# Where TensorE's operands start in SBUF: a two-block transformer kernel on one Trainium2 core

## The chip, the core and the metric

The kernel runs on one core of one Trainium2 chip. Five engines work beside each other there: TensorE (PE in the profile; PEld is its weight load), VectorE (DVE), ScalarE (ACT), GpSimd (POOL) and the queue engine SyncE (SP), and transfers run on 16 DMA engines. The metric is the device time of one execution in microseconds; less is better. A difference of under 0.2% can't be told from no change here.

## What is computed

Two transformer blocks on 256 tokens of width 1024, in float32. The reference, cut to its skeleton:

```python
# block 1
h = rmsnorm(x, g1); parts = split(h @ w_in)            # 1024 -> 6416 columns
att = sliding_window_attention(q, k, v, sinks) @ w_branch_attn
hm = mlstm_chunkwise(...) @ w_branch_mlstm
x = x + (sigmoid(ga) * att + sigmoid(gm) * hm) @ w_out
x = x + peer_ffn(rmsnorm(x, g2), ...)                  # 128 of 16384 experts for each token
# block 2
p = split(rmsnorm(x, g3) @ w_in_2)                     # 1024 -> 5632 columns
x = x + (sigmoid(gs) * stick_breaking(p) + sigmoid(gh) * hgrn2(p)) @ w_out
hn = rmsnorm(x, g4)
x = x + (silu(hn @ w_gate) * (hn @ w_up)) @ w_down     # hidden width 2816
```

`peer_ffn` picks 16 experts for each of 8 heads and each token, takes the dot product of the token with the expert's row of `expert_down`, and adds up the rows of `expert_up` weighted by gate and gelu.

## The kernel before

**Dense products.** Every product with a weight matrix is made in three TensorE passes over operands in the format float32r: a float32 value is split into a rounded part (`hi`) and the rest (`lo`), and `mm3` (L119 to L125) adds up weights-lo times activations-hi, weights-hi times activations-lo and hi times hi. Each weight tile of 512 KB (128 partitions by 1024 values, 4096 bytes in each partition) goes through `stream` (L111): a DMA from SyncE's queue into `raw` (3 buffers), ScalarE rounds it into `hi` (4 buffers, L105), and VectorE or GpSimd, by a pattern of letters (`lo_pat`), writes `lo` (3 buffers, L109).

A matmul has two operands in SBUF: a stationary one of 128 columns, which a weight load puts into the array (the engine called PEld), and a moving one, which streams past it. The weights of the next matmul are loaded while the present one streams. There are two ways of using them:

- `proj_tok_steps` (token-major): the activations are stationary and the weights move, 512 columns a matmul. The profile names such a matmul `acc<-lo,T1h 128x512`. A weight tile has 12 of them. The stages are q, the values, `w_out`, the mixer's inputs of block 2, and the last product `w_fd`.
- `proj_feat_steps` (feature-major): the weights are stationary and the activations move, 256 columns a matmul. The profile names such a matmul `acc<-T1l,hi 128x256`. A weight tile has 24 of them. The stages are the gates, the branch products, the PEER query and the two first products of the FFN (`w_fg`, `w_fu`).

I call them wide (512 columns) and narrow (256 columns). The program has 1056 narrow ones on `fhTh`/`fhTl` (FFN), 1152 on `T1h`/`T1l` (six projections of 192 each, 1152 in all), 192 on `aTh`/`aTl`, 192 on `hmTh`/`hmTl` (the same memory, by tag), 192 on `rTh`/`rTl` (PEER query), and 192 on `oTh`/`oTl`: 2976. Of wide ones 264 have `fTh`/`fTl` stationary, the others `T1h`/`T1l`.

**The gather in the middle.** For PEER, `experts` (L780 on) gathers for one expert of all 128 tokens a tile `ga` (1 MB, 8192 bytes in each partition) by an indirect DMA of GpSimd, 256 times, into ten buffers. VectorE makes the dot product (L794), ScalarE a diagonal matrix `dg` (L800), and TensorE adds up `dg` times the second half of `ga` (L803, float32).

**Order and memory.** The instructions' order on each engine is set by the framework's scheduler from the program's order and priorities. Tiles come from pools; pools are laid out in SBUF one after another in the order in which they are opened, and tiles within a pool in the order of their first use. So the size of any tile moves all tiles that come after it. The built program gives these starts of the tiles in their partitions, in bytes modulo 256:

| tile | role | before | after the change |
|---|---|---|---|
| `hi`, `lo`, feature-major | stationary | 192 | 64 |
| `hi`, `lo`, token-major | moving | 192 | 0 |
| `T1h`, `T1l`, `fhTh`, `fhTl` | moving (narrow), stationary (wide) | 192 | 0 |
| `aTh`, `aTl`, `hmTh`, `hmTl` | moving (narrow) | 32 | 0 |
| `rTh`, `rTl` | moving (narrow) | 160 | 128 |
| `oTh`, `oTl` | moving (narrow) | 128 | 0 |
| `fTh`, `fTl` | stationary (wide) | 96 | 0 |
| `ga` / `dg` | moving / stationary of L803 | 160 / 160 | 0 / 0 |

Slices of these tiles start at multiples of 512 bytes from the tile's start.

Of the kernel before, what the change touches and what calls it, by code (L numbers as in the profile page):

```python
# [10 lines left out]
F32 = mybir.dt.float32  # L11
F32R = mybir.dt.float32r
# [9 lines left out]
P = 128  # L22
D = 1024
KD = D // P
# [6 lines left out]
W_O = (22, 23, 25)  # L31
RAWB, HIB, LOB = 3, 4, 3
NWARM = 9
EB, GB = 4, 10
PI2 = 2.0 * math.pi


# [2 lines left out]
for _n, _w in (("g1", 8), ("g2", 8), ("g3", 8), ("g4", 8), ("lb0", 4), ("lb1", 4), ("ib", 1), ("fb", 1),  # L40
               ("invf", 8), ("sink", 16), ("qg", 64), ("kg", 64), ("qg2", 64), ("kg2", 64), ("hg", 128)):
    _SM[_n] = (_o, _o + _w)
    _o += _w
SMW = _o


@with_exitstack
def peer_hybrid_kernel(ctx: ExitStack, tc: tile.TileContext, A: dict, out: bass.AP, dbg=None, stop=None):
# [15 lines left out]

    warm = st.tile([P, 512], BF, tag="lo", name="warm", bufs=LOB)
    V.memset(warm, 0.0)
    wa = kp.tile([P, 2], F32, name="wa")
    G.memset(wa, 0.0)
    S.activation(wa[:, 0:1], wa[:, 1:2], AF.Copy)
    x = kp.tile([P, 2, D], F32, name="x", tag="xs")  # L70
# [37 lines left out]
            cnt[0] += 1  # L108
        return (V if eng == "v" else G).tensor_tensor(dst_l, src, dst_h.bitcast(F32), op=ALU.subtract)  # L109

    def stream(src, n=1024):  # L111
        raw = st.tile([P, n], F32, tag="raw", name="raw", bufs=RAWB)
        hi = st.tile([P, n], F32R, tag="hi", name="hi", bufs=HIB)
        lo = st.tile([P, n], F32R, tag="lo", name="lo", bufs=LOB)
        with tc.high_priority(offset=PRIO):
            nc.sync.dma_start(raw, src)
            split(hi, lo, raw)
        return hi, lo
# [25 lines left out]
    def proj_feat_steps(w, n, xh, xl, KT, evac, nm=4, tag="acc", kc0=0):  # L144
        acc = [bank(tag) for _ in range((nm + 1) // 2)]
        kp_ = 8 // nm
        for kc in range(KT // kp_):
            hi, lo = stream(w[n, kc0 + kc])
            hi = hi.rearrange("p (k n) -> p k n", k=kp_)
            lo = lo.rearrange("p (k n) -> p k n", k=kp_)  # L150
            for m in range(nm):
                o = acc[m // 2][:, (m % 2) * 256:(m % 2) * 256 + 256]
                ms = slice(m * P, m * P + P)
                for k2 in range(kp_):
                    k = kc * kp_ + k2
                    mm3(o, hi[:, k2, ms], lo[:, k2, ms], xh[:, k], xl[:, k], k == 0 and m % 2 == 0,
                        k == KT - 1 and (m % 2 == 1 or m == nm - 1))
            if kc < KT // kp_ - 1:
                yield
        for m2 in range(len(acc)):  # L160
            evac(m2, acc[m2])
        yield
# [161 lines left out]
    with ExitStack() as c1:  # L324
# [5 lines left out]
        def ten(shape, name, bufs=1, dt=F32, tag=None):  # L330
            return b1.tile(shape, dt, tag=tag or name, name=name, bufs=bufs)

        hTh, hTl = t1()
        n1 = Norm(x, par("g1"), b1, hTh, hTl, ("s4", 3))
        n1.half(0)
# [128 lines left out]
        dump("kT", kT)  # L464


        attTh = ten([P, KD, 256], "aTh", dt=F32R)
        attTl = ten([P, KD, 256], "aTl", dt=F32R)
        nsink = ten([P, 16], "nsink")
        V.tensor_scalar(nsink, par("sink"), -1.0, None, op0=ALU.mult)  # L470
        for tt in range(2):
# [191 lines left out]


    with ExitStack() as c2:
        wp = c2.enter_context(tc.tile_pool(name="wp", bufs=1))
        gp = c2.enter_context(tc.tile_pool(name="gp", bufs=1))
        lo_pat[0] = "p"
        keys = wp.tile([P, 8, P], F32, name="keys")
        nc.scalar.dma_start(keys, A["peer_keys"])  # L670
# [111 lines left out]
        def experts(tt, h, r0, EB):  # L782

            if uacc[tt][0] is None:
                uacc[tt] = [bank("acc") for _ in range(2)]
            s_ = gp.tile([P, EB], F32, name="s_", bufs=3)
            dg = gp.tile([P, EB, P], F32, name="dg", bufs=2)
            rows = []
            for j in range(EB):
                ga = gp.tile([P, 2 * D], F32, name="ga", bufs=GB)  # L790
                G.indirect_dma_start(ga, None, A["peer_du"], bass.IndirectOffsetOnAxis(  # L791
                    idx[tt][h][:, r0 + j:r0 + j + 1], 0))
                jk = gp.tile([P, D], BF, name="jk", bufs=1)
                dot = V.scalar_tensor_tensor(jk, ga[:, 0:D], 1.0, xn[:, tt], op0=ALU.mult, op1=ALU.mult,  # L794
                                             accum_out=s_[:, j:j + 1])
                rows.append(ga)
            S.activation(s_, s_, AF.Gelu)
            V.tensor_tensor(s_, s_, gate[tt][h][:, r0:r0 + EB], op=ALU.mult)
            for j in range(EB):
                S.activation(dg[:, j], ident, AF.Copy, scale=s_[:, j:j + 1])  # L800
            for dh in range(2):
                for j in range(EB):
                    T.matmul(uacc[tt][dh], dg[:, j], rows[j][:, D + dh * 512:D + dh * 512 + 512],  # L803
                             start=h + r0 + j == 0, stop=h == 7 and r0 + j == 15)
            return dot
# [28 lines left out]
    with ExitStack() as c4:  # L834
        b2 = c4.enter_context(tc.tile_pool(name="b2", bufs=1))

        def ten(shape, name, bufs=1, dt=F32, tag=None):
            return b2.tile(shape, dt, tag=tag or name, name=name, bufs=bufs)

        def head_norm2(src, nh, hd, gain, tag):  # L840
            sv = src.rearrange("p (h d) -> p h d", h=nh)
# [55 lines left out]
        qs, ks, vs = (ten([P, 2, 512], nm_) for nm_ in ("qs", "ks", "vs"))  # L897
        vh = ten([P, 2, 512], "vh", tag="qs")
        gg = ten([P, 2, 512], "gg", tag="ks")
        oTh = ten([P, KD, 256], "oTh", dt=F32R)  # L900
        oTl = ten([P, KD, 256], "oTl", dt=F32R)
        qT2 = ten([P, 4, 256], "qT2")
        kT2 = ten([P, 4, 256], "kT2")
        attn = ten([P, 2, 4, P], "attn")
# [197 lines left out]
    with ExitStack() as c5:  # L1102
        fp = c5.enter_context(tc.tile_pool(name="fp", bufs=1))
        hTh = fp.tile([P, KD, 256], F32R, name="fhTh")
        hTl = fp.tile([P, KD, 256], F32R, name="fhTl")
        n4 = Norm(x, par("g4"), fp, hTh, hTl)
        for n in range(2):
            cs_ = slice(n * 512, (n + 1) * 512)
# [2 lines left out]
            n4.half(n)  # L1111
        n4.factor(row=False)
        dump("x4", x)
        NF = 22
        fTh = fp.tile([P, NF, 256], F32R, name="fTh")
        fTl = fp.tile([P, NF, 256], F32R, name="fTl")
        for n in range(6):
            nm = 4 if n < 5 else 2
            got = []
# [113 lines left out]
```

## Time and profile before

| | us |
|---|---|
| median of 3 runs (lowest, highest) | 1396.51 (1396.5, 1397.77) |
| the profiled execution | 1393.9 |
| its span, first to last instruction | 1392.1 |
| TensorE busy | 1228.3 (88%) |
| VectorE / GpSimd / ScalarE busy | 891.0 / 567.7 / 515.3 |

The profiled execution's time is 1.8 us more than its span, and 2.6 us less than the median of the runs. A matmul's duration in the profile is the time from its start to the end of its result, and matmuls overlap: the next one starts long before the former ends. What counts in a run of matmuls is the time from one start to the next, which I call the pitch. It is worked out from a view that counts the instructions in a stretch: since those that stick out at the stretch's edges are counted too, the pitch is (stretch + one duration) / count.

### The profile page before, as it was taken

The numbers are of one execution on the slowest core, as the hardware profiler recorded it, in microseconds if no ns is written. First come the engines' busy times: TensorE is split into PE (matmuls) and PEld (weight loads), VectorE is DVE, ScalarE is ACT, GpSimd is POOL, SyncE is SP. The second block draws the span as 40 slices with busy tenths as digits, with TensorE's granted clock in tenths as the row PEclk, the third lists the DMA queues.
The fourth block names the chain that finished last, engine by engine and source line by source line (L and its number), as shares of the span: only waits on it lengthen the run. The fifth ranks groups of instructions, "written<-read, shape, count | busy, mean of one in ns | idle before, by whom it ended". The sixth has DMA issues, their size and how long they took to land.

```text
span 1392.1 us, 16704 instructions
## 1 busy us (share of the span) xinstructions
PE 1228.3 (88%) x5785; PEld 849.9 (61%) x5785; DVE 891.0 (64%) x1963; ACT 515.3 (37%) x927; POOL 567.7 (41%) x394
## 2 busy tenths in 40 slices
PE   8999999994888777878777786878999999999998
PEld 6976789993333333333333332333888999899987
DVE  6966658558576776666867766665699786442521
ACT  6465434452122222112322211221474564544442
POOL 3321412543535444444434454453100005578764
PEclk9999999995889889989988999999999999999999
DMA  6543325666999999999999999999355335465564
GB/s 215 168 134 107 121 92 169 186 191 265 421 421 421 419 421 416 421 419 412 408 419 419 416 422 411 415 409 411 116 163 167 106 107 181 153 189 176 188 190 136
DMA packets 69779, 383.53 MB, mean 276 GB/s; under 512 B 8000, under 2 KB 8512, under 8 KB 36928
## 3 DMA queue, kind: packets, MB, share of 16 engines
q0 software_dynamic: 36864, 268.45, 46.8%
q1 hardware_dynamic: 31968, 112.11, 26.1%
q10 hardware_dynamic: 864, 1.90, 0.4%
q8 instruction: 46, 0.75, 0.2%
q14 instruction: 37, 0.30, 0.1%
HBM read 381.39 MB, written 1.05 MB: 275 GB/s over the span
## 4 chain that ended last, share of the span: by engine, by line
PE 45%; DMA 24%; DVE 16%; issue 7%; POOL 6%; ACT 1%; POOLq 0%; SPq 0%; ACTq 0%; DVEq 0%
DMA ga<-in_peer_du_dram,idx 22%; PE acc L121 11%; PE acc L124 11%; PE acc L125 10%; POOL ga L791 5%; DVE jk L794 5%; PE acc L803 2%; PE sm L124 2%; PE sm L125 2%; PE sm L121 2%; PE sm L489 1%; PE sm L1052 1%; PE s L514 1%; DVE lo L109 1%; ACT hi L105 1%
## 5 line engine op out<-in xcount | busy, mean ns | idle before, releaser
L803 PE MATMUL acc<-ga,dg 128*128 128x512 f32 x1024 | 509.3, 657 | 145.1 <-ACT dg L800 144.9
L803 PEld LDWEIGHTS acc<-ga,dg 128*128 128x128 f32 x1024 | 210.6, 210 | 442.7 <-issue 252.8
L791 POOL DMA_INDIRECT ga<-in_peer_du_dram,idx x256 | 297.3, 1161 | 361.7 <-PE acc L803 236.6
L794 DVE SCALAR_TENSOR_TENSOR jk<-ga,xn 128x1024 bf16<-128x1024 f32 x256 | 313.4, 1224 | 199.9 <-DMA ga<-in_peer_du_dram,idx 199.6
L109 POOL TENSOR_TENSOR lo<-raw,hi 128x1024 fp32r<-128x1024 f32 (+1 forms) x88 | 216.8, 2467 | 392.9 <-PE acc L125 258.2
L105 ACT ACTIVATE hi<-raw 128x1024 fp32r<-128x1024 f32 (+1 forms) x210 | 220.3, 1051 | 256.6 <-PE acc L125 75.2
L109 DVE TENSOR_TENSOR lo<-raw,hi 128x1024 fp32r<-128x1024 f32 (+1 forms) x122 | 157.8, 1294 | 105.4 <-PE acc L124 35.1
L121 PE MATMUL acc<-T1l,hi 128*128 128x256 f32 x384 | 109.8, 287 | 0.3 <-DVE T1l L237 0.3
L124 PE MATMUL acc<-T1h,lo 128*128 128x256 f32 x384 | 109.9, 286 | 0.0
L125 PE MATMUL acc<-T1h,hi 128*128 128x256 f32 x384 | 109.3, 285 | 0.0
L121 PE MATMUL acc<-lo,T1h 128*128 128x512 f32 (+1 forms) x256 | 99.8, 395 | 3.3 <-DVE lo L109 3.0
L124 PE MATMUL acc<-hi,T1l 128*128 128x512 f32 (+1 forms) x256 | 99.9, 391 | 0.7 <-DVE T1l L306 0.6
L125 PE MATMUL acc<-hi,T1h 128*128 128x512 f32 (+1 forms) x256 | 99.6, 390 | 0.0
L121 PEld LDWEIGHTS acc<-T1l,hi 128*128 128x128 f32 x384 | 73.3, 191 | 1.8 <-issue 0.7
L124 PEld LDWEIGHTS acc<-T1h,lo 128*128 128x128 f32 x384 | 73.4, 191 | 1.0 <-issue 0.5
L125 PEld LDWEIGHTS acc<-T1h,hi 128*128 128x128 f32 x384 | 73.4, 191 | 0.9 <-issue 0.4
L121 PEld LDWEIGHTS acc<-lo,T1h 128*128 128x128 f32 x256 | 48.7, 192 | 12.9 <-DVE lo L109 3.5
L124 PEld LDWEIGHTS acc<-hi,T1l 128*128 128x128 f32 x256 | 49.0, 191 | 11.9 <-DVE T1l L306 1.9
L125 PEld LDWEIGHTS acc<-hi,T1h 128*128 128x128 f32 x256 | 48.9, 191 | 10.2 <-issue 1.0
L125 PE MATMUL sm<-fhTh,hi 128*128 128x256 f32 x176 | 49.6, 283 | 0.0
L124 PE MATMUL sm<-fhTh,lo 128*128 128x256 f32 x176 | 49.6, 283 | 0.0
L124 PE MATMUL acc<-fhTh,lo 128*128 128x256 f32 x176 | 49.6, 283 | 0.0
(849 smaller groups left out, 1995.1 us busy)
## 6 DMA issues: line engine op xcount, KB each, us to landing
raw<-in_w_in_dram SPq DMA_DIRECT2D x92, 512.0 KB, 3.5
raw<-in_w_fg_dram SPq DMA_DIRECT2D x22, 512.0 KB, 3.6
raw<-in_w_fu_dram SPq DMA_DIRECT2D x22, 512.0 KB, 3.7
raw<-in_w_fd_dram SPq DMA_DIRECT2D x22, 512.0 KB, 3.8
raw<-in_w_out_dram SPq DMA_DIRECT2D x16, 512.0 KB, 3.6
raw<-in_w_ba_dram SPq DMA_DIRECT2D x8, 512.0 KB, 3.5
raw<-in_w_bm_dram SPq DMA_DIRECT2D x8, 512.0 KB, 4.0
raw<-in_peer_wq_dram SPq DMA_DIRECT2D x8, 512.0 KB, 3.5
```

The source lines that it names most:

```text
L105: S.activation(dst_h, src, AF.Copy)
L109: return (V if eng == "v" else G).tensor_tensor(dst_l, src, dst_h.bitcast(F32), op=ALU.subtract)
L121: m = T.matmul(o, lh, rl, start=start, stop=False)
L124: T.matmul(o, ll, rh, start=False, stop=False)
L125: return T.matmul(o, lh, rh, start=False, stop=stop)
L489: T.matmul(b[:, (i - i0) * W:(i - i0 + 1) * W], qT[pr, h // 2, tt * P:(tt + 1) * P], kT[pr, g, 0:W], start=False, stop=i == i0 + per - 1)
L514: T.matmul(po[pr, :], kv[:, sb, P + g * 64:P + g * 64 + 64], pT, start=sb == 0, stop=sb == tt)
L791: G.indirect_dma_start(ga, None, A["peer_du"], bass.IndirectOffsetOnAxis(idx[tt][h][:, r0 + j:r0 + j + 1], 0))
L794: dot = V.scalar_tensor_tensor(jk, ga[:, 0:D], 1.0, xn[:, tt], op0=ALU.mult, op1=ALU.mult, accum_out=s_[:, j:j + 1])
L803: T.matmul(uacc[tt][dh], dg[:, j], rows[j][:, D + dh * 512:D + dh * 512 + 512], start=h + r0 + j == 0, stop=h == 7 and r0 + j == 15)
L1052: T.matmul(b[:, tt * 4 + m], xl_[:, m, tt], xr_[:, m, tt, :, 1], start=tt + m == 0, stop=tt + m == 4)
```

## The change

It moves no work between engines, and adds none. It sets the byte positions of TensorE's operands:

- The tiles `wa` and `s_` are made 32 columns wide (only the first columns are used), and the parameter tile `sm` is rounded up to a multiple of 64 columns, so that the tiles behind them start at multiples of 256 bytes. `s_` gets a fourth buffer.
- `attTh`/`attTl`, `oTh`/`oTl` and `fTh`/`fTl` are allocated ahead of the other tiles of their pools, and the pool `gp` of the gather is opened ahead of `wp`.
- Each `hi` and `lo` buffer is 64 values (256 bytes) longer, and a feature-major product uses the part that starts 16 values, which is 64 bytes, behind the buffer's start.

```diff
-EB, GB = 4, 10
+EB, GB, OFF = 4, 10, 64
...
-SMW = _o
+SMW = -(-_o // 64) * 64
...
-    wa = kp.tile([P, 2], F32, name="wa")
+    wa = kp.tile([P, 32], F32, name="wa")
...
-    def stream(src, n=1024):
+    def stream(src, n=1024, shift=0):
         raw = st.tile([P, n], F32, tag="raw", name="raw", bufs=RAWB)
-        hi = st.tile([P, n], F32R, tag="hi", name="hi", bufs=HIB)
-        lo = st.tile([P, n], F32R, tag="lo", name="lo", bufs=LOB)
+        hi = st.tile([P, 1024 + OFF], F32R, tag="hi", name="hi", bufs=HIB)[:, shift:shift + n]
+        lo = st.tile([P, 1024 + OFF], F32R, tag="lo", name="lo", bufs=LOB)[:, shift:shift + n]
...
-            hi, lo = stream(w[n, kc0 + kc])
+            hi, lo = stream(w[n, kc0 + kc], shift=16)
...
+        attTh = ten([P, KD, 256], "aTh", dt=F32R)
+        attTl = ten([P, KD, 256], "aTl", dt=F32R)
...
+        gp = c2.enter_context(tc.tile_pool(name="gp", bufs=1))
         wp = c2.enter_context(tc.tile_pool(name="wp", bufs=1))
-        gp = c2.enter_context(tc.tile_pool(name="gp", bufs=1))
...
-            s_ = gp.tile([P, EB], F32, name="s_", bufs=3)
+            s_ = gp.tile([P, 32], F32, name="s_", bufs=4)[:, 0:EB]
...
+        oTh = ten([P, KD, 256], "oTh", dt=F32R)
+        oTl = ten([P, KD, 256], "oTl", dt=F32R)
...
+        NF = 22
+        fTh = fp.tile([P, NF, 256], F32R, name="fTh")
+        fTl = fp.tile([P, NF, 256], F32R, name="fTl")
```

TensorE's instructions stand in the same order as before throughout; so do GpSimd's and SyncE's. Near the start, where the cosines of the rotary embedding (`cs`) are made, the scheduler exchanges some rows on VectorE and ScalarE. On ScalarE, where `T1h` are the last parts of the first normed activations, `junk,nss` the squares for their norm, and `hi` the first weight tiles, it stands thus before:

```order
L218 ACTIVATE T1h<-sm 128x256 x2
L105 ACTIVATE hi<-raw 128x1024
L218 ACTIVATE T1h<-sm 128x256
L243 ACTIVATE junk,nss<-x 128x512 x3
L396 ACT_TABLE_LOAD
L396 ACTIVATE cs<-ang 128x32
L243 ACTIVATE junk,nss<-x 128x512
```

And in the changed kernel (its lines are two to four higher there):

```order
L220 ACTIVATE T1h<-sm 128x256 x2
L106 ACTIVATE hi<-raw 128x1024
L400 ACT_TABLE_LOAD
L400 ACTIVATE cs<-ang 128x32
L220 ACTIVATE T1h<-sm 128x256
L245 ACTIVATE junk,nss<-x 128x512 x4
```

The table load and the cosines have moved ahead of the last part of `T1h`.

## Rows read from the trace of the kernel before

**Rows 1.** The page: busy time, and the span in 40 slices.

```profile
PE 1228.3 (88%) x5785; PEld 849.9 (61%) x5785; DVE 891.0 (64%) x1963; ACT 515.3 (37%) x927; POOL 567.7 (41%) x394
...
PE   8999999994888777878777786878999999999998
...
PEclk9999999995889889989988999999999999999999
DMA  6543325666999999999999999999355335465564
```

**Rows 2.** The page: chain that ended last, first line, and the gather's DMA queue.

```profile
q0 software_dynamic: 36864, 268.45, 46.8%
...
PE 45%; DMA 24%; DVE 16%; issue 7%; POOL 6%; ACT 1%; POOLq 0%; SPq 0%; ACTq 0%; DVEq 0%
```

**Rows 3.** Stretches: each engine's busy us and count, granted clock, DMA share, GB/s.

```profile
core 0: us, PE busy (x) PEld busy (x) DVE busy (x) ACT busy (x) POOL busy (x), PEclk, DMA share, GB/s
141.00:189.00 48.00, 46.76 (x290) 36.01 (x288) 27.11 (x39) 19.93 (x34) 16.36 (x7) 1.00 0.33 100
244.00:266.00 22.00, 22.00 (x186) 22.00 (x185) 9.86 (x12) 10.03 (x11) 9.14 (x4) 1.00 0.57 175
309.00:315.00 6.00, 6.00 (x53) 6.00 (x52) 5.93 (x7) 4.04 (x5) 0.00 (x0) 1.00 0.37 120
400.00:900.00 500.00, 392.19 (x802) 162.59 (x801) 341.19 (x913) 113.69 (x310) 230.67 (x199) 0.91 1.01 417
999.00:1008.00 9.00, 9.00 (x77) 9.00 (x76) 5.39 (x5) 5.00 (x6) 3.38 (x2) 1.00 0.57 177
1010.00:1025.00 15.00, 15.00 (x68) 12.43 (x67) 12.83 (x21) 11.54 (x13) 1.05 (x1) 1.00 0.57 163
1077.00:1149.00 72.00, 72.00 (x563) 67.63 (x562) 55.03 (x99) 40.41 (x48) 1.98 (x1) 1.00 0.36 109
1151.00:1171.00 20.00, 20.00 (x179) 20.00 (x178) 11.05 (x13) 9.02 (x11) 11.03 (x5) 1.00 0.60 190
1218.00:1326.00 108.00, 108.00 (x902) 108.00 (x901) 44.14 (x36) 49.79 (x57) 86.06 (x41) 1.00 0.58 183
1330.00:1386.00 56.00, 56.00 (x242) 45.05 (x241) 9.42 (x8) 19.11 (x18) 31.54 (x14) 1.00 0.56 169
```

**Rows 4.** Groups by form on PE: 1151 to 1171 us, then one of 1218 to 1326 us.

```profile
L121 PE MATMUL acc<-oTl,hi 128*128 128x256 f32 x60 | 16.6, 276 | 0.0
...
L124 PE MATMUL sm<-fhTh,lo 128*128 128x256 f32 x157 | 44.3, 283 | 0.0
```

**Rows 5.** Timeline of PE in order of time: start, us, instruction, [idle before <-releaser].

```profile
228.01 0.55 PE L275 MATMUL sm<-cst,hm 128*128 128x128 f32 x3 [0.99 <-DVE hm L655]
...
308.00 0.68 PE L261 MATMUL sm<-cst,nr 128*128 128x128 f32 x4 [1.09 <-DVE nr L195]
...
1207.39 0.28 PE L125 MATMUL acc<-fhTh,hi 128*128 128x256 f32 x1
1210.68 0.57 PE L261 MATMUL sm<-cst,nr 128*128 128x128 f32 x3 [3.02 <-DVE nr L195]
```

**Rows 6.** Groups by form on PE: the first of 1331 to 1351 us and of 1010 to 1025 us.

```profile
L124 PE MATMUL acc<-hi,fTl 128*128 128x512 f32 x29 | 11.6, 399 | 0.0
...
L124 PE MATMUL acc<-hi,T1l 128*128 128x512 f32 x23 | 9.0, 389 | 0.0
```

**Rows 7.** The page: GpSimd's lo group, and the landing time of FFN weights.

```profile
L109 POOL TENSOR_TENSOR lo<-raw,hi 128x1024 fp32r<-128x1024 f32 (+1 forms) x88 | 216.8, 2467 | 392.9 <-PE acc L125 258.2
...
raw<-in_w_fg_dram SPq DMA_DIRECT2D x22, 512.0 KB, 3.6
```

**Rows 8.** Timeline around 20 us: ScalarE, then VectorE, then PE.

```profile
18.17 0.47 ACT L218 ACTIVATE T1h<-sm 128x256 fp32r<-128x256 f32 x1
...
20.50 1.28 ACT L396 ACT_TABLE_LOAD   x1
21.79 0.23 ACT L396 ACTIVATE cs<-ang 128x32 f32<-128x32 f32 x1
...
20.57 0.47 DVE L219 SCALAR_TENSOR_TENSOR T1l<-sm,T1h 128x256 fp32r<-128x256 f32 x1
...
21.83 0.41 PE L121 MATMUL acc<-lo,T1h 128*128 128x272 f32 x2
```

More of the change, by code (lines that the diff above doesn't have):

```diff
@@ L464, in peer_hybrid_kernel @@
         dump("kT", kT)
-        attTh = ten([P, KD, 256], "aTh", dt=F32R)
-        attTl = ten([P, KD, 256], "aTl", dt=F32R)
         nsink = ten([P, 16], "nsink")
@@ L899, in peer_hybrid_kernel @@
         gg = ten([P, 2, 512], "gg", tag="ks")
-        oTh = ten([P, KD, 256], "oTh", dt=F32R)
-        oTl = ten([P, KD, 256], "oTl", dt=F32R)
         qT2 = ten([P, 4, 256], "qT2")
@@ L1113, in peer_hybrid_kernel @@
         dump("x4", x)
-        NF = 22
-        fTh = fp.tile([P, NF, 256], F32R, name="fTh")
-        fTl = fp.tile([P, NF, 256], F32R, name="fTl")
         for n in range(6):
```

## The prediction

> **What bounds the kernel now.** I read the page's busy line and slices first, then the chain, then a table of stretches. TensorE is busy for 88% of the span, and its slices show 9 except in the middle, where the DMA slices show 9 instead [rows 1]. The chain says the same: PE 45%, DMA 24%, and DVE 16% [rows 2]. So there are two regimes. In the slices where DMA shows 9 (roughly 350 to 970 us) the gather runs: 400 to 900 us has a DMA share of 1.01 at 417 GB/s [rows 3], and a faster TensorE gains nothing there. Outside it TensorE is the bound: the stretches of 22, 20, 108 and 56 us in the branch product, its counterpart in block 2, the FFN and `w_fd` have PE busy for all of their time at a granted clock of 1.00, and even the interleaved stretches have 46.76 of 48 us and 72.00 of 72 us [rows 3]. Time taken from a matmul's pitch there is time taken from the kernel, unless it falls ahead of a wait.
>
> The pitch differs between matmuls that do the same work. For narrow ones, (stretch + one duration) / count, from [rows 3] with durations of 0.28 us [rows 4]:
>
> - 1218 to 1326 us, `fhT`: 108.283 / 902 = 120.0 ns. Moving operand at 192 and weights at 192 modulo 256: distance 0.
> - 999 to 1008 us, `T1`: 9.283 / 77 = 120.6 ns. Distance 0 too.
> - 244 to 266 us, `hmT`: 22.28 / 186 = 119.8 ns. Moving at 32, weights at 192: distance 160.
> - 309 to 315 us, `rT`: 6.28 / 53 = 118.5 ns. Moving at 160: distance 32.
> - 1151 to 1171 us, `oT`: 20.276 / 179 = 113.3 ns. Moving at 128: distance 64.
>
> Shape, passes, clock and source of the weights are the same in all five; what differs is where the operands start. The one stretch whose weights lie 64 bytes behind the moving operand is 6.7 ns a matmul faster than the two with distance 0. Wide ones show a difference too: `fT` (stationary at 96, moving at 192) has 56.4 / 242 = 233.0 ns, `T1` (both at 192) 15.39 / 68 = 226.3 ns [rows 3, 6].
>
> **The change, part by part.** After it, narrow products on `T1`, `fhT`, `aT`, `hmT` and `oT` have the moving operand at 0 and weights at 64, the distance of the 113.3 ns stretch; every wide one has distance 0, that of the 226.3 ns stretch; `rT` has moving 128, weights 64, a distance no row shows.
>
> *FFN, narrow:* 1056 x (120.0 - 113.3) = 7.1 us. *`aT` and `hmT`:* 384 x 6.5 = 2.5 us, the `hmT` row standing for both. *`T1`, narrow:* 1152, half of them in the two interleaved stretches 141 to 189 and 1077 to 1149 us, where 290 and 563 matmuls stand for 192 and 384 narrow ones [rows 3], so that some pairs are broken up by other work. I take 6.7 ns for the closed half (3.9 us) and 85% of it for the other (3.3 us): 7.2 us. *`oT`:* already at distance 64, nothing. *`rT`:* distances 32 and 160 cost nearly the same, as if the pattern came back every 128 bytes; then the new distance of -64 acts like 64 and gives 5.2 ns. Bounds are the two ends seen, 113.3 and 120.6: between +1.0 and -0.4 us for 192. But what is gained ahead of 308 us is waited away (below), so I take 0.3 us. *`w_fd`, wide:* 264 x (233.0 - 226.3) = 1.8 us. Wide products on `T1` keep their distance: nothing. So does L803 in the gather (160/160 becomes 0/0). Sum: 7.1 + 2.5 + 7.2 + 0.3 + 1.8 = 18.9 us.
>
> *What is waited away.* TensorE waits three times for a chain on VectorE that doesn't get faster. At 1210.68 us the spreading of the fourth norm's factor waits for `nr` since 1207.39 us, with 3.02 us idle [rows 5]; some 100 narrow matmuls stand ahead of it after `w_out2`, and their 0.7 us only lengthens that wait. At 308.00 us the same happens with the second norm [rows 5] and takes what `rT` gains in its first 18 us. At 228.01 us TensorE waits 0.99 us for `hm` [rows 5]: up to 0.5 us from the 75 narrow ones ahead. I take off 1.2 us for these, and 0.5 us for side work in the two interleaved stretches that may come late when its cover shrinks by some 6%. Sum: 18.9 - 1.7 = 17.2 us.
>
> *Supply of the weights.* A weight tile then lasts 24 x 113.3 = 2.72 us instead of 2.88. GpSimd's `lo` takes 2.47 us [rows 7], and in the FFN it does two of three tiles: 4.9 of every 8.16 us. With its other work GpSimd is busy for 86.06 of 108 us [rows 3], which would have to fit into 102. The `oT` stretch already ran at 2.72 us a tile with no idle time [rows 4]. The transfer, 3.6 us to landing [rows 7] with three buffers, asks for 512 KB in 2.72 us, 193 GB/s against the 417 the gather moved. So I price supply at nothing; what hides it is that four `hi` and three `lo` buffers let both be made two tiles ahead.
>
> *The exchanged rows at the start.* The last `T1h` (18.17 us) now follows a table load of 1.28 us and `cs` of 0.23 us, so it ends near 20.1 us. Its partner `T1l` started only at 20.57 us anyway, and TensorE comes to those parts at 21.83 us or later [rows 8]. Cost nothing; without that cover 1.5 us.
>
> *The rest.* The longer `sm` load and `wa` memset are a few bytes at the start, bounded by 0.1 us either way; the fourth `s_` buffer lies in the gather. VectorE, ScalarE and GpSimd read and write at other positions too; no row shows their durations to depend on it, and they have slack outside the gather.
>
> Here a rule of the Trainium skill stands against the change. The page "SBUF — State Buffer", section "Who interferes with whom", gives TensorE two read ports, one for the moving operand and one for the weight load, calls them independent, and says that PE and ACT never wait on anyone. By that the distance couldn't matter and the sum would be 0. The trace disagrees: 113.3 against 120.0 ns at the same clock [rows 3].
>
> **The rivals.**
>
> *The position counts, not the distance.* The 113.3 ns has been seen at moving 128, weights 192 alone. If it is tied to these places, moving 0 with weights 64 may cost 120 as now: narrow products gain nothing, `w_fd` perhaps nothing either: 1395 to 1397 us. For it: only one stretch shows the fast pitch, and it is also the one stretch with four instead of eight k-steps. Against: `T1` at 192 and `hmT` at 32 are at very different places with the same pitch, and the two wide pitches differ with distance as well. The skill's rule on independent ports would end here too.
>
> *Slower: an unseen pair of places with a higher pitch.* Same mechanism, other sign: if moving 0 with weights 64 cost 125 ns, 5 ns over the closed stretches, 2592 x 5 = 13 us are added, the 192 of `oT` lose 192 x 11.7 = 2.2 us, and `w_fd` gives 1.8 back: 1410 us. It decides at a mean narrow pitch of about 120.0 ns. Against it: no stretch in [rows 3] has over 120.6 ns at the full clock.
>
> *A supply or side chain takes over half of it.* If GpSimd's `lo` or the side chains of the interleaved stretches come late, the FFN and those stretches keep half their gain: 1396.5 - 9 = 1388 us. For it: GpSimd's 80% in the FFN. Against it: `oT` above.
>
> *The gather gets faster.* Its packets of 8192 bytes now start at 160 modulo 256 and then at 0. If the part of a 256-byte block ahead of the start is moved as well, a packet moves 8352 bytes now and 8192 then, 1.9%. The gather's queue holds the 16 engines for 46.8% of 1392.1 = 651 us [rows 2]: 12.5 us less, 1367 us in all. Against it: the start matters only if it counts on the written side, and no row has an aligned destination to compare. The rule is in the Trainium skill, page "DMA: Bandwidth & Descriptors", section "How a descriptor splits into AXI transactions", which tells it of reads that start off a 256-byte boundary; no run here shows it.
>
> **How the numbers follow.** The sum is made on the profiled execution (1393.9 us, span 1392.1): 1393.9 - 17.2 = 1376.7 us there. The runs' median lies 2.6 us above that execution, so the forecast for the median is 1396.5 - 17 = 1379.5 us. Its own range is 1376 (all 18.9 us, `rT` in full) to 1384 us. Chances: forecast 0.77; half taken by supply or side chains 0.08; position, not distance 0.06; gather faster 0.05; slower 0.04. The range reaches to the supply case and down a little for what the gather or the small float32 matmuls may give: 1373 to 1389 us, which leaves out 0.15. About 0.2% (2.8 us) is what a measurement of this kernel can tell from no change: faster 0.90, same 0.06, slower 0.04.
>
> **What would show it.** In the FFN the counts of a stretch must give 113 to 114 ns a narrow matmul, with durations near 276 instead of 283 ns; so in 244 to 266 us and in the gate products; `w_fd` must show 226 to 227 ns. The idle time before L261 in the FFN must grow from 3.02 to about 3.7 us. The gather must start some 6 us earlier and last as long as before. Pitches still at 120 would refute the distance; fast pitches with new idle time on TensorE would mean supply; a shorter gather would be the packets.

## The result, and the profile after

| | before | after the change |
|---|---|---|
| median of the runs, us | 1396.68 | 1373.96 |
| lowest to highest, us | 1396.5 to 1397.77 | 1372.99 to 1379.99 |
| the profiled execution, its span | 1393.9, 1392.1 | 1372.99, 1371.2 |
| TensorE busy | 1228.3 | 1202.5 |

The ratio of the times is 0.9853, with an interval of 0.9837 to 0.9869, which is 18 to 23 us less; the two medians differ by 22.7 us. Forecast were 17. The sign is the one predicted. The time lies inside the predicted range of 1373 to 1389 us, but only 1 us above its lower end, and below the forecast's own range of 1376 to 1384 us. The sum came out near by two misses of opposite sign, and that is what the rest of this document is about.

First the page of the changed kernel: busy times, three of its rows of slices, the gather's queue and the first line of the chain.

```profile
PE 1202.5 (88%) x5785; PEld 832.8 (61%) x5785; DVE 894.8 (65%) x1963; ACT 514.4 (38%) x927; POOL 565.6 (41%) x394
...
PE   8999999994977778788877777887999999999998
...
PEclk9999999995899989899999999999999999999999
DMA  7533335666999999999999999999355335556554
...
q0 software_dynamic: 36864, 268.45, 46.7%
...
PE 44%; DMA 29%; DVE 17%; issue 4%; POOL 4%; ACT 1%; POOLq 0%; DVEq 0%; SPq 0%; ACTq 0%
```

The picture is that of [rows 1, 2]: TensorE outside, the DMA engines in the middle. The shares hide what changed, because everything shrank alike. The stretches tell more (columns as in [rows 3]; times are shifted by what was gained ahead of them):

```profile
core 0: us, PE busy (x) PEld busy (x) DVE busy (x) ACT busy (x) POOL busy (x), PEclk, DMA share, GB/s
141.00:187.00 46.00, 44.61 (x279) 33.99 (x278) 25.78 (x36) 18.58 (x32) 15.95 (x7) 1.00 0.33 104
241.00:262.00 21.00, 21.00 (x187) 21.00 (x187) 10.14 (x12) 10.08 (x12) 9.42 (x4) 1.00 0.59 181
305.00:310.00 5.00, 5.00 (x45) 5.00 (x44) 4.69 (x6) 4.20 (x5) 0.00 (x0) 1.00 0.35 100
400.00:900.00 500.00, 389.58 (x812) 162.23 (x812) 346.39 (x936) 115.07 (x312) 231.54 (x201) 0.92 1.01 423
988.00:997.00 9.00, 9.00 (x79) 9.00 (x78) 5.65 (x5) 5.00 (x6) 3.34 (x2) 1.00 0.61 175
1066.00:1136.00 70.00, 70.00 (x562) 65.67 (x561) 54.57 (x99) 40.07 (x48) 2.00 (x1) 1.00 0.34 111
1205.00:1306.00 101.00, 101.00 (x892) 100.83 (x890) 45.23 (x36) 48.18 (x56) 84.29 (x39) 1.00 0.61 193
1310.00:1366.00 56.00, 55.88 (x247) 45.93 (x246) 12.44 (x9) 19.96 (x20) 34.24 (x15) 1.00 0.52 171
```

With (stretch + one duration) / count, and 0.28 us for a narrow matmul: the FFN has 101.28 / 892 = 113.5 ns (120.0 before), `hmT` 21.28 / 187 = 113.8 (119.8). But `T1` at 988 us has 9.28 / 79 = 117.5 ns (120.6), at the very same distance of 64 bytes, and `rT` 5.28 / 45 = 117.3 (118.5). `w_fd` has 56.39 / 247 = 228.3 ns (233.0). And in the 500 us of the gather the line counts 812 matmuls at 423 GB/s where [rows 3] has 802 at 417: the gather runs faster, which the sum had at nothing.

The groups of these stretches (first the FFN's, then `w_fd`'s), in the same form as [rows 4, 6], show durations of 277 ns in place of 283 and 389 in place of 399:

```profile
L126 PE MATMUL sm<-fhTh,lo 128*128 128x256 f32 x153 | 42.1, 277 | 0.0
...
L127 PE MATMUL acc<-hi,fTh 128*128 128x512 f32 x30 | 11.7, 389 | 0.0
```

Where the time went (us). A stage is taken from the start of its first matmul to the start of its last:

| stretch of the program | before | after | gain |
|---|---|---|---|
| start to the first gathered packet | 329.0 | 325.2 | 3.8 |
| of it `aT` and `hmT` | 51.2 | 48.9 | 2.3 |
| first to last gathered packet | 647.5 | 638.9 | 8.6 |
| last packet to the end | 415.6 | 407.1 | 8.5 |
| of it last packet to the first `T1` product | 8.6 | 10.3 | -1.7 |
| of it narrow `T1` (985 and 1076 us before) | 96.9 | 94.6 | 2.3 |
| of it FFN, narrow, with its wait | 131.1 | 124.7 | 6.4 |
| of it `w_fd` | 61.4 | 60.1 | 1.3 |

### The profile page after: what moved, and what is told of

Read it like the earlier page. It is cut to its first block, busy times and chain, and to the rows that moved or that the text cites. A ratio compares the mean times of both kernels' runs of the same rounds, so it can differ in the third digit from the quotient of the medians.

```text
span 1371.2 us, 16704 instructions
## 1 busy us (share of the span) xinstructions
PE 1202.5 (88%) x5785; PEld 832.8 (61%) x5785; DVE 894.8 (65%) x1963; ACT 514.4 (38%) x927; POOL 565.6 (41%) x394
## 3 DMA queue, kind: packets, MB, share of 16 engines
q1 hardware_dynamic: 31968, 112.15, 25.9%
## 4 chain that ended last, share of the span: by engine, by line
PE 44%; DMA 29%; DVE 17%; issue 4%; POOL 4%; ACT 1%; POOLq 0%; DVEq 0%; SPq 0%; ACTq 0%
DMA ga<-in_peer_du_dram,idx 28%; PE acc L123 10%; PE acc L126 10%; PE acc L127 10%; DVE jk L796 6%; POOL ga L793 3%; PE acc L805 2%; PE sm L126 1%; PE sm L123 1%; PE sm L127 1%; POOL lo L110 1%; PE sm L491 1%; DVE lo L110 1%; PE sm L1055 1%; PE s L516 1%
## 5 line engine op out<-in xcount | busy, mean ns | idle before, releaser
L805 PE MATMUL acc<-ga,dg 128*128 128x512 f32 x1024 | 497.9, 645 | 149.6 <-ACT dg L802 149.6
L805 PEld LDWEIGHTS acc<-ga,dg 128*128 128x128 f32 x1024 | 206.9, 207 | 439.5 <-issue 242.7
L793 POOL DMA_INDIRECT ga<-in_peer_du_dram,idx x256 | 292.1, 1141 | 356.0 <-PE acc L805 207.1
L110 DVE TENSOR_TENSOR lo<-raw,hi 128x1024 fp32r<-128x1024 f32 (+1 forms) x122 | 163.1, 1338 | 94.0 <-ACT hi L106 36.2
L127 PEld LDWEIGHTS acc<-hi,T1h 128*128 128x128 f32 x256 | 49.1, 192 | 10.3 <-issue 1.0
```

The lines of the kernel that those rows point to most:

```text
L127: return T.matmul(o, lh, rh, start=False, stop=stop)
```

## Experiments

The medians of the kernel before were 1395.28, 1393.94, 1393.45 and 1395.11 us in the four series; each ratio below is against the runs of its own series.

**1. The gather's tiles alone.** Of the changed kernel, only `ga` and `dg` are moved back to 160 modulo 256, by two small unused tiles; every other start stays.

```diff
             s_ = gp.tile([P, 32], F32, name="s_", bufs=4)[:, 0:EB]
+            gp.tile([P, 40], F32, name="pad1", bufs=1)
             dg = gp.tile([P, EB, P], F32, name="dg", bufs=2)
...
+                gp.tile([P, 24], F32, name="pad2", bufs=1)
                 jk = gp.tile([P, D], BF, name="jk", bufs=1)
```

> The changed kernel with one thing put back: the gather's tiles ga and dg start at 160 modulo 256 again, all else as changed. Theory 'packets' (a gathered packet of 8192 bytes takes longer when its destination starts off a 256-byte block): mean packet time back from 312 to 317 ns, the gather's transfers from 639 to some 647 us, the whole some 8.6 us slower than the changed kernel, 1382 us. Rival 'chance' (the gather was shorter for another reason, such as when TensorE frees the buffers): gather stays at 639 us, whole at 1374 us.

Measured: 1381.2 us, ratio 0.9893 (0.9871 to 0.9916). A second kernel has 32 columns in both unused tiles, so that `ga` and `dg` start at 128:

> The changed kernel with ga and dg at 128 modulo 256. If a packet pays for starting off a 256-byte block, it pays here as at 160: gather 647 us, 1382 us. If it pays only for starting off a 64-byte step (160 is off one, 128 is not): gather 639 us, 1374 us.

Measured: 1383.95 us, 0.9912 (0.9886 to 0.9939). And the reverse, the kernel before with `ga` and `dg` at 0 (24 and 40 columns), and nothing else changed:

> The kernel before with one part of the change alone: the gather's tiles ga and dg start at 0 modulo 256 instead of 160; everything else stands where it stood. Theory 'packets': mean packet time 317 to 312 ns, gather 647 to 639 us, whole 8 to 9 us faster than before, ratio 0.994. Rival 'the packets need the rest of the change too (xn, jk or the weights' raw tiles on 256)': gather stays at 647 us, ratio 1.000.

Measured: 1386.88 us, 0.9947 (0.993 to 0.9965). All four cases and the kernel before, from the view of the DMA queues between 400 and 900 us (packets, MB, share of 16 engines); first the kernel before, `ga` at 160:

```profile
q0 software_dynamic: 28600, 208.32, 101.0%
```

Then the changed kernel, at 0:

```profile
q0 software_dynamic: 29005, 211.18, 100.8%
```

The changed kernel with `ga` at 160:

```profile
q0 software_dynamic: 28555, 207.94, 100.9%
```

The same with `ga` at 128:

```profile
q0 software_dynamic: 28563, 208.04, 100.7%
```

The kernel before with `ga` at 0:

```profile
q0 software_dynamic: 28992, 211.15, 100.8%
```

The engines are full in all five, and the packets fall into two groups: 28,990 to 29,010 where `ga` starts at 0, 28,560 to 28,600 where it starts at 160 or 128. From first to last packet the gather takes 638.9 and 638.4 us in the first group, 647.5, 648.4 and 648.0 in the second. The other profiles fall the same way: 637.8 to 640.5 us at 0, and 647.1 us in experiment 3, at 160. By the packets' own records, one of 8192 bytes takes 311.8 ns on average in the first group, 98% of them 309; in the second 315.9 to 316.7 ns, most between 309 and 321. The 256 gathers have 32,768 of these packets, 2048 for each engine if they are spread evenly, and 2048 x 4.9 ns = 10.0 us, of which the gather's length shows 8.6. So the start of the *destination* in SBUF counts for a DMA, and 128 is no better than 160. The tiles `ga` and `dg` were moved together; that the packets themselves got shorter, with the engines full, points to `ga`.

**2. The weights of narrow products back at distance 0.** All tiles stay aligned:

```diff
-            hi, lo = stream(w[n, kc0 + kc], shift=16)
+            hi, lo = stream(w[n, kc0 + kc], shift=0)
```

> The changed kernel without the 64 bytes: weights of narrow products start at 0 as their moving operand does (distance 0), all else as changed. Theory 'distance': narrow pitch 120.0 ns in the FFN (fhT), in the branch product (hmT) and now also in the product on oT, which had 113.3 before and after; whole some 9 to 14 us slower than the changed kernel, 1383 to 1388 us. Rival 'position' (the fast pitch belongs to places at a multiple of 256): pitches stay at 113 to 118 ns and the time at 1374 us.

Measured: 1386.0 us, 0.9933 (0.9911 to 0.9954). The stretches of `hmT`, `oT`, the FFN and `w_fd` in it:

```profile
245.00:265.00 20.00, 20.00 (x169) 20.00 (x168) 9.22 (x11) 8.48 (x9) 7.17 (x4) 1.00 0.56 176
...
1142.00:1162.00 20.00, 20.00 (x169) 20.00 (x169) 10.16 (x12) 8.17 (x11) 10.97 (x5) 1.00 0.58 184
...
1205.00:1310.00 105.00, 105.00 (x878) 105.00 (x877) 38.59 (x34) 49.49 (x56) 83.88 (x40) 1.00 0.56 177
...
1320.00:1376.00 56.00, 56.00 (x249) 46.37 (x248) 9.41 (x8) 19.92 (x20) 33.76 (x15) 1.00 0.54 176
```

The narrow ones have 20.28 / 169 = 120.0, 120.0 and 105.28 / 878 = 119.9 ns: `oT`, which had 113.3 before the change, is now as slow as the others. The wide ones of `w_fd` keep 56.39 / 249 = 226.5 ns. The gather (638.8 us) and `w_fd` make up what is left of the gain. So some 11 to 12 us hang on the 64 bytes: 1386.0 against the 1373.96 and 1373.58 us of the changed kernel in two other series is 12, the ratios 0.9933 against 0.9853 and 0.9858 are 11.

**3. The shift alone, in the kernel before.** Activations stay at 192, 32, 160 and 128; the weights of narrow products go from 192 to 0.

```diff
-    def stream(src, n=1024):
+    def stream(src, n=1024, shift=0):
...
-        hi = st.tile([P, n], F32R, tag="hi", name="hi", bufs=HIB)
-        lo = st.tile([P, n], F32R, tag="lo", name="lo", bufs=LOB)
+        hi = st.tile([P, 1024 + 64], F32R, tag="hi", name="hi", bufs=HIB)[:, shift:shift + n]
+        lo = st.tile([P, 1024 + 64], F32R, tag="lo", name="lo", bufs=LOB)[:, shift:shift + n]
...
-            hi, lo = stream(w[n, kc0 + kc])
+            hi, lo = stream(w[n, kc0 + kc], shift=16)
```

> The kernel before with the other part alone: narrow products use their weights 64 bytes behind the buffer's start, so at 0 modulo 256, while all moving operands stay at their old places (T1 and fhT 192, aT and hmT 32, rT 160, oT 128). Theory 'distance': T1 and fhT (now 64) at 113 or 118 ns, hmT (224) near 118, oT (128) slower than before, near 118.6 instead of 113.3; gather unchanged at 647 us; whole some 9 to 12 us faster than before, ratio 0.992. Rival 'position': oT stays at 113.3 ns and T1 and fhT at 120.

Measured: 1387.04 us, 0.9933 (0.9908 to 0.9957). Its stretches of `T1` (distance 64 now), `hmT` (224), `oT` (128) and `w_fd` (stationary 96, moving 192, as before):

```profile
42.00:64.00 22.00, 21.99 (x195) 21.82 (x194) 20.98 (x43) 11.47 (x14) 8.91 (x3) 1.00 0.62 190
...
244.00:262.00 18.00, 18.00 (x156) 18.00 (x155) 8.82 (x10) 8.21 (x9) 5.70 (x4) 1.00 0.61 178
...
1146.00:1165.00 19.00, 19.00 (x163) 19.00 (x162) 10.10 (x12) 7.56 (x9) 10.16 (x5) 1.00 0.62 186
...
1330.00:1380.00 50.00, 50.00 (x216) 40.24 (x215) 7.42 (x7) 16.89 (x16) 27.96 (x12) 1.00 0.55 172
```

`T1` is faster with its moving operand still at 192: 22.28 / 195 = 114.3 ns with the interruptions, 113.3 in its undisturbed parts. `oT`, which did not move, got slower, 19.28 / 163 = 118.3 ns, because its weights moved away from it. `hmT` has 117.2, `w_fd` its old 233.3. That is distance, not position. The whole gained 6.9 us where I had expected 9 to 12: the FFN of this kernel, at distance 64 too, ran at 117.8 ns behind its wait, to which I come back in 5.

**4. Which distances.** Two kernels with another shift in each of the FFN's twelve narrow products and in both halves of `w_fd`; each gave one time, 1378.4 and 1378.02 us.

```diff
+        SEQ = [16, 0, 4, 8, 12, 20, 24, 28, 32, 40, 48, 56]
...
-                proj_feat(A["w_fu"], n, hTh, hTl, KD, ev_up, tag="sm")
+                proj_feat(A["w_fu"], n, hTh, hTl, KD, ev_up, tag="sm", shift=SEQ[2 * n + 1])
...
-            proj_tok(A["w_fd"], n, fTh, fTl, NF, ev)
+            proj_tok(A["w_fd"], n, fTh, fTl, NF, ev, shift=[16, 32][n])
```

> The changed kernel with another distance (weights minus moving operand, in bytes) in each of the FFN's twelve narrow products, in this order: 64, 0, 16, 32, 48, 80, 96, 112, 128, 160, 192, 224; and in the two halves of w_fd the moving weights 64 and 128 bytes behind the stationary activations. Theory 'distance, repeating every 128 bytes': 0 and 128 at 120 ns, 64 and 192 at 113 or 118 ns, 32, 96, 160 and 224 between; w_fd at 226.7 ns with 128 and other than that with 64. Rival 'repeating every 256 bytes': 128 and 192 have pitches of their own. Time between 1374 and 1380 us.

> The changed kernel with fine steps of the distance in the FFN's twelve narrow products, in this order: 64, 56, 72, 60, 68, 52, 76, 4, 44, 84, 64, 24 bytes; and w_fd with its moving weights at 224 and 192, a distance of the stationary from the moving operand of 32 and 64. Theory 'an even distance of 64 is a special place': 113.3 ns at 64 alone, 115 to 120 at its neighbours, and wide ones over 226.7 ns at 32 and 64. Rival 'a basin': 113 to 114 ns for several neighbours of 64 too. Time 1374 to 1380 us.

The mean time from start to start in each product, its first 20 matmuls left out:

| weights behind the moving operand, bytes modulo 256 | ns a narrow matmul |
|---|---|
| 52, 76 | 113.3, 113.3 |
| 64 (three products) | 113.6, 113.6, 113.3 |
| 4, 16, 24, 32, 44, 48 | 118.3, 118.3, 118.6, 118.4, 117.8, 117.8 |
| 56, 60, 68, 72 | 117.9, 119.6, 118.3, 118.3 |
| 80, 84, 96 | 118.7, 120.1, 117.3 |
| 0, 112, 160 | 120.0, 120.1, 120.1 |
| 128, 192, 224 | 118.6, 117.8, 117.8 |

Two fences with stretches of these products, first 112 bytes in the first kernel, then 72, 52 and 76 bytes in the second. In 8 us stand 69, 70 and 73 matmuls, 8.28 us / count = 120.0, 118.3 and 113.4 ns; for 76 bytes it is 7.28 / 64 = 113.8:

```profile
1268.00:1276.00 8.00, 8.00 (x69) 8.00 (x69) 1.22 (x1) 2.21 (x3) 7.78 (x5) 1.00 0.38 125
```

```profile
1211.00:1219.00 8.00, 8.00 (x70) 8.00 (x69) 2.68 (x2) 3.24 (x4) 5.37 (x4) 1.00 0.64 211
...
1245.00:1253.00 8.00, 8.00 (x73) 8.00 (x72) 0.35 (x1) 3.00 (x5) 7.78 (x5) 1.00 0.58 173
1257.00:1264.00 7.00, 7.00 (x64) 7.00 (x63) 1.92 (x2) 2.52 (x4) 5.09 (x3) 1.00 0.57 163
```

In these products no distance but 52, 64 and 76 shows 113. Distance 128 (118.6) is not like distance 0 (120.0), so the pattern does not simply come back after 128 bytes, as I had taken for `rT`; but 192, at 117.8 here, shows 113.3 too in another profile, as experiment 5 tells. For wide ones, stationary behind moving: 192 gives 229.0 ns, 128 232.4, 64 233.4, 32 233.3; of those tried only 0 (226.8 in experiment 2) is fast. Narrow and wide matmuls want different distances.

But a single product each can't be read as a curve: 56 and 60 beside 52 and 64 look odd, and they should. The next runs tell why.

**5. The same program again, and the two neighbours that looked as fast.** The changed kernel with nothing altered, then with its weights 52 and 76 bytes off in place of 64 (`shift=13`, `shift=19`).

> The changed kernel once more, unaltered, to see whether a stage settles at the same pitch in every execution. Theory 'two settled pitches at 64, picked by the moment at which a stage starts': some stages with distance 64 that ran at 113.3 ns now run at 118, or the other way, with nothing changed in the program; an FFN at 118 costs 1056 x 4.7 = 5 us, so executions spread over 1372 to 1380 us. Rival 'the program fixes it': every stage at the same pitch as in the first profile, spread under 2 us.

> The changed kernel with the weights of narrow products 52 bytes off instead of 64. Theory '52 has the fast pitch alone': T1, aT, hmT, oT and fhT all at 113.3 ns, rT (then at 180) unlike that; the time at or under the fastest of the changed kernel, 1370 to 1373 us, with a smaller spread. Rival 'two settled pitches here too': some stages at 118, time 1373 to 1380 us.

> The changed kernel with the weights of narrow products 76 bytes off instead of 64. The same two theories as for 52 bytes: all narrow stages but rT at 113.3 ns and 1370 to 1373 us, or a mixture of 113 and 118 and 1373 to 1380 us.

Measured: 1373.58 us (0.9858, 0.9834 to 0.9881; single times 1370.38 to 1378.83), 1372.71 (0.9842, 0.9824 to 0.986) and 1374.0 (0.9861, 0.9845 to 0.9877). Three stretches of the unaltered kernel's second profile, whose execution took 1377.83 us: FFN ahead of its wait, just behind it, and the rest of the FFN:

```profile
1183.00:1192.00 9.00, 9.00 (x81) 9.00 (x81) 3.61 (x10) 7.34 (x15) 4.80 (x2) 1.00 0.56 151
1196.00:1201.00 5.00, 5.00 (x23) 5.00 (x24) 1.71 (x3) 1.58 (x3) 1.92 (x2) 0.50 0.35 105
...
1205.00:1306.00 101.00, 101.00 (x860) 101.00 (x859) 41.48 (x34) 47.97 (x54) 81.60 (x39) 1.00 0.59 186
```

Ahead of the wait the matmuls have 9.28 / 81 = 114.6 ns with an interruption, and 113.3 in the undisturbed part. Behind it the granted clock is 0.50, the lower of its two levels (1.2 of 2.4 GHz), for about 5 us: 213 ns a matmul for 22 matmuls, 2.1 us in all. And when the clock is back, the FFN does not return to 113.3 but runs at 101.28 / 860 = 117.8 ns to its end: the same program, the same distance, and 4 us more. The wait itself is the same in both executions. Timeline of TensorE around it, in the first profile of the changed kernel (start, us, and the idle time before with its releaser):

```profile
1197.19 0.68 PE L263 MATMUL sm<-cst,nr 128*128 128x128 f32 x4 [3.22 <-DVE nr L197]
1197.63 0.37 PE L123 MATMUL sm<-fhTl,hi 128*128 128x256 f32 x1
1197.83 0.28 PE L126 MATMUL sm<-fhTh,lo 128*128 128x256 f32 x1
```

and in the second:

```profile
1195.96 1.19 PE L263 MATMUL sm<-cst,nr 128*128 128x128 f32 x4 [3.21 <-DVE nr L197]
1196.81 0.56 PE L123 MATMUL sm<-fhTl,hi 128*128 128x256 f32 x1
1197.16 0.41 PE L126 MATMUL sm<-fhTh,lo 128*128 128x256 f32 x1
```

After 3.22 us idle the clock stayed, after 3.21 us it fell (0.28 us a matmul against 0.41). Of all thirteen profiles it fell behind this wait in five of the eight in which the wait has 3.21 or 3.22 us, and in one of the five in which it has 2.87 to 3.02 us; the kernel before, at 3.02, is not among them. That one is the second kernel of experiment 4, its wait and the granted clock behind it:

```profile
1195.80 0.74 PE L263 MATMUL sm<-cst,nr 128*128 128x128 f32 x2 [2.87 <-DVE nr L197]
...
1196.00:1199.00 3.00, 3.00 (x15) 3.00 (x16) 1.72 (x3) 1.50 (x3) 0.11 (x1) 0.50 0.56 175
```

In the unaltered kernel's second profile, and with `ga` at 160, the clock also fell at 153.7 us, behind 1.39 us idle, and the interleaved stretch that begins at 140 us took 48.9 us in both where the first profile, after the same wait, has 47.3. So the length of the wait alone does not decide it.

So a stretch of narrow matmuls at distance 64 settles on one of two pitches, 113.3 or 117.8, keeps it until something interrupts it (a wait, or other work of TensorE between its matmuls), and may leave the interruption on the other. Settled pitches of one closed stretch each, that is one with little such work, in four profiles with `T1`, `hmT`, `oT` and `fhT` at distance 64 (ns):

| | `T1` 42 us | `hmT` | `T1` behind the gather, start and end | `oT` | FFN behind its wait |
|---|---|---|---|---|---|
| changed kernel, first profile | 117.8 | 113.3 | 117.8, 117.8 | 113.3 | 113.3 |
| second profile | 113.3, then 117.8 | 113.3 | 117.8, 113.3 | 113.3 | 117.8 |
| `ga` at 160 | 117.8 | 117.8 | 113.3, 117.8 | 113.3 | 113.3, at the end 117.8 |
| `ga` at 128 | 117.8 | 113.3 | 117.8, 113.3 | 113.3 | 113.3 |

At 52 bytes the two are 113.3 (FFN, `oT`) and 120.0 (`hmT`, which had 113.3 at 64). Its stretches of `hmT` and of the FFN have 21.28 / 178 = 119.6 and 95.28 / 841 = 113.3 ns:

```profile
241.00:262.00 21.00, 21.00 (x178) 21.00 (x177) 8.96 (x11) 9.22 (x11) 7.35 (x4) 1.00 0.57 170
1205.00:1300.00 95.00, 95.00 (x841) 95.00 (x840) 36.33 (x34) 47.09 (x53) 69.94 (x38) 1.00 0.63 196
```

At 76 every closed stretch but `rT` settled at 113.3. And `rT`, whose weights lie 64 bytes ahead of the moving operand in the changed kernel (distance 192), has the same two pitches as distance 64: 117.8 in the first profile, and in the second 117.8 up to 304 us and 113.3 from 306 us on. Its stretch there has 6.28 / 55 = 114.2 ns with the interruption:

```profile
306.00:312.00 6.00, 6.00 (x55) 6.00 (x54) 5.55 (x7) 4.42 (x5) 0.00 (x0) 1.00 0.46 109
```

A last kernel asks whether 76 bytes has only the one pitch: all narrow products at 76, `rT` too (`shift=51` there, whose moving operand starts at 128).

> The weights of every narrow product lie 76 bytes behind its moving operand, now those of the PEER query too (which stood at 76 - 128 = -52 bytes, 204 modulo 256, and had some 120 ns a matmul with the others at 76). Theory A, a distance of 76 bytes has one settled pitch, 113.3 ns, where 64 bytes have two, 113.3 and 117.8: in this second profile at 76 again every closed stretch (T1 from 42 us on, hmT, the T1 products behind the gather, fhT) settles at 113.3, and rT too; rT's stage gets 192 x 6 = 1.2 us shorter, part of which is waited away ahead of nr; time 1372.5 to 1374, spread under 4 us. Theory B, 76 bytes only happened to fall on the faster of two pitches in its one profile: at least one closed stretch settles above 116 ns, and the spread of the runs is as wide as at 64 bytes (7 to 8 us).

Measured: 1373.61 us, 0.9855 (0.9834 to 0.9877), 1372.89 to 1377.71. The FFN and `hmT` have 95.28 / 837 = 113.8 and 21.28 / 187 = 113.8 ns:

```profile
1205.00:1300.00 95.00, 95.00 (x837) 94.76 (x836) 45.16 (x34) 45.37 (x52) 78.44 (x37) 1.00 0.60 194
241.00:262.00 21.00, 21.00 (x187) 21.00 (x187) 10.52 (x13) 10.46 (x12) 7.48 (x4) 1.00 0.65 197
```

`rT` settles at 113.3 where it had 120.0 and 123.3 with the others at 76. The rest of the closed stretches settle at 113.3 too, but for some 35 matmuls at 228 to 232 us, which run at 120.0 between two interruptions. So in its two profiles 76 has the slower pitch less often than 64, is not free of it, and the time is no better. Part of the reason stands in the first stage, where both kernels at 76 bytes have TensorE wait 2.3 us, and no other profile as much as 0.2 us. Timeline of TensorE, of VectorE, and of GpSimd in this kernel:

```profile
62.46 1.07 PE L465 MATMUL sm<-cst,q 128*128 128x128 f32 x8 [2.31 <-DVE rsa L196]
```

```profile
57.98 0.68 DVE L579 TENSOR_TENSOR mqT<-acc,nrow 128x512 f32<-128x512 f32 x1
58.59 3.33 DVE L110 TENSOR_TENSOR lo<-raw,hi 128x1024 fp32r<-128x1024 f32 x1
61.84 0.28 DVE L442 TENSOR_TENSOR q<-rp0q,rp1q 128x128 f32<-128x128 f32 x1
```

```profile
58.45 2.38 POOL L110 TENSOR_TENSOR lo<-raw,hi 128x1024 fp32r<-128x1024 f32 x1 [5.74 <-PE acc L127]
```

VectorE's `lo`, which takes 1.2 us elsewhere, takes 3.33 us here (3.13 in the other kernel at 76). In the changed kernel's first profile `lo` was just through, and the instruction of 0.2 us three places further (`rsa`, L196) has 2.38 us, from 59.77 us on. VectorE stops for some 2.1 us in both; where the stop falls on `lo`, `rsa` comes later, and TensorE waits for it. The stop goes with GpSimd's own `lo`. Here that began at 58.45 us, 0.14 us ahead of VectorE's `lo`, and ended at 60.83; VectorE's `lo` ended 1.1 us later, about the time that it takes by itself. In the eleven profiles of the kernels that do not use 76 bytes GpSimd's `lo` began behind VectorE's, and the long `rsa` ended 0.03 or 0.04 us after GpSimd's `lo` in every one. So VectorE stands there until GpSimd's `lo` is through, and the 2.3 us at 76 bytes go with which of the two began first; why the order differs is not shown.

## Why the prediction was right, and where it was not

**Distance, not position: right.** Experiment 3 gave `T1` 113.3 ns at moving 192 and weights 0, and took the fast pitch away from `oT` without moving `oT`; experiment 2 has 120.0 ns at 0 and 0, the value of 192 and 192. The rival "position" is refuted. The Trainium skill (page "SBUF — State Buffer", section "Who interferes with whom") calls TensorE's two reads independent; the trace disagrees, with 120.0 against 113.3 ns in the same products. By what mechanism the distance counts is not shown.

**FFN: right in this profile.** 131.1 to 124.7 us, 6.4 less, where 7.1 less some 0.7 waited away were forecast. In the second profile, which has the lower clock and then 117.8 ns behind the wait, it is 131.3 us, no gain. So what I took for a property of the program is one of two outcomes. The spread of the times after, 1373 to 1380 us, is as wide as that term; but the kernel before spreads by 1.3 to 5.8 us in its series as well, so the spread is not shown to come from the pitches alone.

**`aT` and `hmT`: right.** 2.5 us forecast, 2.3 measured.

**Narrow `T1`: over-sized.** 7.2 us forecast, 3.2 measured in this profile (0.9 ahead of the gather, 2.3 behind it). The step that failed is "6.7 ns for the closed half": at 42 and 974 us these products settled at 117.8 ns, a gain of 2.2 and not 6.7, so each gained 0.4 us and not 1.3. The third closed stretch, at 217 us, ran mostly at 113.3 and gained nothing (25.8 us before, 25.9 after), since TensorE waits for `hm` twice there, 0.31 and 1.56 us, where it waited 0.99 us once:

```profile
216.95 0.44 PE L277 MATMUL sm<-cst,hm 128*128 128x128 f32 x2 [0.31 <-DVE hm L657]
225.65 0.87 PE L277 MATMUL sm<-cst,hm 128*128 128x128 f32 x6 [1.56 <-DVE hm L657]
```

The one row at distance 64 that I had, 20 us of `oT` without an interruption, could show one pitch only.

**`rT`: half right, the term small.** "As if the pattern came back every 128 bytes" does not hold for 0 and 128 (120.0 and 118.6). That -64 acts like 64 fits, but with both pitches of 64: in this profile `rT` kept 117.8 ns and its stage went from 25.3 to 25.5 us, in the second its last part had 113.3.

**`w_fd`: right.** 227.4 ns from start to start (233.3 before, 226.8 in most of the other profiles with distance 0), 1.3 us of the 1.8 forecast; TensorE was idle for 0.12 of 56 us.

**Waits: right in direction.** The wait of L263 grew from 3.02 to 3.22 us, not to 3.7, and that for `hm` from 0.99 to 1.87 in two parts. What I had not asked is what the clock does behind a wait: in six of the thirteen profiles the lower level followed that of L263, at 2.1 us in the one worked out above. So a wait that I had priced at nothing can cost something. That the 0.2 us more bring it about is not shown, for the clock fell behind 2.87 us as well.

**Supply: right.** GpSimd was busy for 84.29 of 101 us in the FFN, and TensorE did not wait for it.

**The gather: wrong.** "Nothing" was the term, and the rival that I gave 0.05 came true beside the forecast: 8.6 us of the 12.5 that I had priced, for a packet of 316.7 ns became 311.8, which is 1.5% and not 1.9%. I had called the written side undecided and then priced it at nothing, though the gather is the longest stretch of the kernel and the change moved exactly its destination. A term bounded by 0 and 12.5 us, with no row to tell the ends apart, should not have stood at one end. That a start off a 256-byte boundary costs a transfer is what the Trainium skill's page "DMA: Bandwidth & Descriptors" (section "How a descriptor splits into AXI transactions") tells of reads; here 311.8 against 316.7 ns show it of the written side. By that section the bytes between the boundary and the start are the cost, which would be, as an estimate, 1.9% at 160 and 1.5% at 128. Measured are 1.5 and 1.3% in the packets, and no difference between the two in the gather's length (647.1 to 648.4 us at 160, 648.0 at 128); whether the loss follows the number of bytes is not shown.

The sum by measured terms, in the profiled executions: 1.0 us ahead of the first narrow products, 3.2 for `T1`, 2.3 for `aT` and `hmT`, -0.2 for `rT`, 8.6 in the gather, -1.7 behind it, 6.4 for the FFN and 1.3 for `w_fd`: 20.9, which is 1393.9 less 1373.0. The TensorE terms alone give 13.0 where 17.2 were forecast. The two odd ones are not shown to be part of the change: the 1.0 us varies from 0.3 to 1.2 between other profiles, and the stretch from the last packet to `T1` has 8.5 to 8.7 us in nine of thirteen profiles, the unaltered kernel's second among them, and 10.0 to 10.3 in four, all of changed kernels. The medians tell the same: alignment of the gather alone gives the kernel before 7.1 us (1393.94 less 1386.88) and the shift alone 6.9 (less 1387.04), and taken out of the changed kernel they cost some 7 (1381.2 against 1373.96 and 1373.58) and 12 us, or 5 and 11 by the ratios; the shift is worth more there, since `aT`, `hmT` and `oT` have the right distance too.

What stays open: what picks the pitch. It changes at interruptions. The fall of the clock alone does not pick it: with `ga` at 128 the clock fell as well, and the FFN then settled at 113.3.

## What to carry to other kernels

Where a kernel is bound by back-to-back matmuls, compare the pitch of stretches with the same shape, and look at where both operands start: with a narrow moving operand and its weights at the same offset modulo 256 a matmul took up to 6% longer here than with the weights 64 or 76 bytes behind, and 2% longer where those settled on their slower pitch of 117.8 ns. Place the destinations of large gathers at multiples of 256 bytes; that took 1.5% off the mean packet here. A pitch read from one profile is one outcome: profile the same program twice before a term of a sum rests on it.

## What the runs showed of the hardware that I had not expected

- Destination of a gather: 98% of the packets of 8192 bytes take 309 ns where the tile starts at a multiple of 256 bytes (311.8 on average), and the average is 316 to 317 at 160 and at 128.
- Two settled pitches for the same instructions at the same distance: 113.3 and 117.8 ns at 64 bytes, 113.3 and 120.0 at 52; at 64 bytes each held for over 800 matmuls on end.
- Narrow matmuls (256 columns) are slow at distance 0 (120.0) and wide ones (512 columns), of the distances tried, fast only there (226.8 against 229.0 to 233.4).
- After the same idle time of 3.2 us TensorE's granted clock was 0.50, the lower of its two levels, for 2 to 5 us of matmuls in one execution of the changed kernel and stayed at 1.00 in another; it also fell behind idle times of 2.87 and 1.39 us.
- VectorE stood still near 60 us until GpSimd's `lo` was through, in all thirteen profiles: its own `lo` took 3.33 and 3.13 us in place of 1.2 where GpSimd's had begun first, elsewhere `rsa` took 2.4 us in place of 0.2.
